# Hybrid S5 and pooling step: stores of ScalarE's results on ScalarE's queue, operands loaded one use ahead, within-chunk products over 128 rows

## The chip, the cores and the metric

The kernel runs on one core of one Trainium2 chip, in one launch. The metric is the device time in microseconds; it is given as the median of three runs. Of these runs one execution is profiled separately, and every row below comes from that execution. TensorE is called PE here, VectorE DVE, ScalarE ACT, GpSimd POOL, and SyncE, which only issues transfers, SP.

## The reference, cut to what matters

One layer works on 128 context tokens and 512 latent tokens (640 in all, D = 1024, float32). Each of 64 S5 groups has 16 channels and 64 complex states in two directions. The part that the change touches computes this:

```
z = h @ w_in + b_in                      # 1024 for S5, 512 for pooling, 2 x 1024 gates
s_t = lam_bar * s_(t-1) + B u_t          # per group, forward and backward
y   = Re(C s) + d * u                    # both directions added
v   = gelu(y_f + y_b);  v = v * sigmoid(v @ w_glu + b_glu)
yb  = pool_mix(u_b) @ w_proj_b
merged = sigmoid(g_a) * (v @ w_proj_a) + sigmoid(g_b) * yb
x = LN(alpha * x + gate * (merged @ w_out + b_out))
```

Then follow a squared-ReLU MLP with its own layer norm, and the outputs: both token sets and the final S5 states of the context.

## The kernel before

All 640 tokens go through every stage together. The S5 recurrence is cut into 80 chunks of 8 tokens (16 chunks of context, 64 of latent tokens). Per group, a matrix product brings the tokens of a chunk into a state input (`in_proj`, with weights that `gen_in` makes), a scan runs over the chunks (`scan_step`), and `out_proj` adds two parts: the state at the chunk's edge through `q`, and the influence of the tokens within the chunk on each other through `tm`. The forward direction stands in partitions 0 to 63 and the backward direction in 64 to 127, in all of these tiles. The backward half works on the chunks in reverse order, so its inputs come from a reversed copy.

The stages in order of time:

- Adaptive layer norm and the first two `w_in` blocks, up to about 45 us.
- S5 generation, about 45 to 165 us. For eight channel blocks m, PE makes the input projection (48 matmuls of 128x320), `ua_evac` lets ACT write it in chunk order to `uj`, and its reversal to `ujr`; both are stored to DRAM (`ud`, `urd`, lines 367 and 371) and loaded back with another layout (`load_u`) for `in_proj`. In between DVE makes the weights `wt` (in `gen_in`, from coefficients `b`) and `q` (in `gen_q`, from coefficients `c`), PE transposes `wt` (line 489), and `gen_t` makes `tm`, by way of DRAM (`sd`).
- Scan, about 165 to 280 us: DVE runs the scan steps, while PE computes the remaining 20 `w_in` blocks (`fill` and `plain`, line 612), whose results `g` ACT writes and SP stores (`ubd`, `gbd`, `gad`).
- Output, about 282 to 384 us: 16 calls of `out_proj(e)`, each four group columns `l`. Between them lie the last three `w_in` blocks in halves (`halves`), the pooling maps (`pool_map`) and the eight projections of the pooling branch (`pool_proj`, one per `e` from 9 on), each multiplied with a stored gate `gb`. `load_out(e + 4)` loads `tm`, `q` and `u`; `load_y` and `gelu` take the result on.
- GLU, projections, output matrix and MLP, from 384 us to the end; the change doesn't touch them.

Weights arrive as 512 KB blocks `wr` (two buffers, line 327), are split by ACT (line 321) and DVE (line 322) into a high and a low part `wh` (three buffers), and each product is made of three passes. PE writes its results to PSUM: two buffers `ps` of two banks, and four single banks.

Each engine works through its own instructions in order. A scheduler sets that order when the program is built, from the order of the code, the buffers and its own estimates; it moves loads ahead as far as their buffers allow. Before the change every transfer of this part except those of POOL is issued by SP, in one line: an issue that waits holds all that stand behind it. Transfers of SP and ACT use eight completion counters in turn, so that each also waits for the one eight places before it.

In `out_proj`, per column, two state products (real and imaginary part, `i` = 0 and 1) and the within-chunk product (`i` = 2) are each made twice, for the upper and the lower 64 rows, into two PSUM banks; the second bank is reversed in chunk order when it is added.

Of the kernel before, what the change touches and what calls it, by code (L numbers as in the profile page):

```python
# [17 lines left out]
P = 128  # L18
# [3 lines left out]
KT = 8  # L22
TC = 8
NC = NT // TC
# [14 lines left out]
def hybrid_kernel(ctx: ExitStack, tc: tile.TileContext, xin, cc, w_ada0, w_ada, w_in, w_glu, w_pa, w_pool, w_pb,  # L39
                  w_out, w_m1, w_m2, cols, rows, brow, lam, bpk, cpk, ddg, s0, cst, invc, out, nstate):  # L40
    nc = tc.nc
    V, S, T = nc.vector, nc.scalar, nc.tensor
# [318 lines left out]
    def ua_evac(m, ps):  # L361

        uj = half([P, TC, NC], "uj")
        S.activation(uj[:, ::-1, :].rearrange("p j (n c) -> p j n c", n=2),
                     v2(ps).rearrange("p n (c j) -> p j n c", j=TC),
                     AF.Identity, bias=colt[:, C_BIN + m:C_BIN + m + 1])
        dma(ud[m].rearrange("j p c -> p j c"), uj)
        ur = half([P, TC, NC], "ujr")
        S.copy(ur[:, :, 0:CP], uj[:, :, CP - 1::-1])
        S.copy(ur[:, :, CP:NC], uj[:, :, NC - 1:CP - 1:-1])  # L370
        dma(urd[m].rearrange("j p c -> p j c"), ur)

# [89 lines left out]
    us, bs = {}, [None]  # L462

    def load_u(m):
# [6 lines left out]
        return us_  # L471

    def gen_in(e):

        if e % 2 == 0:
            b = bs[0] = bt([P, 8, 3, 16], "b")
            dma(b[:, :, 0:2, :].rearrange("p (a l) r i -> p a l r i", a=2), bpk[:, e:e + 2])
            V.tensor_tensor(b[:, :, 2, :], b[:, :, 0, :], b[:, :, 1, :], op=ALU.add)
            V.tensor_tensor(b[:, :, 1, :], b[:, :, 1, :], b[:, :, 0, :], op=ALU.subtract)
# [52 lines left out]
    def gen_q(m):  # L532

        c = c3t([P, 8, 3, 16], "c")
        dma(c[:, :, 0:2, :].rearrange("p (a l) r i -> p a l r i", a=2), cpk[:, 2 * m:2 * m + 2])
        V.tensor_tensor(c[:, :, 2, :], c[:, :, 0, :], c[:, :, 1, :], op=ALU.add)
# [32 lines left out]
    def load_out(e):  # L569
# [9 lines left out]
        u = ut([P, 4, NC], "u")  # L579
        for hf, d in enumerate((ud, urd)):  # L580
            dma(u[64 * hf:64 * hf + 64], d[m, 4 * hf:4 * hf + 4].rearrange("j (i g) c -> (j i) g c", g=8)
                [:, (e % 2) * 4:(e % 2) * 4 + 4, :])
        outs[e] = q, u

    def out_proj(e):
# [5 lines left out]
        for l in range(4):  # L591
            for i in range(3):
                for hf in range(2):
                    d = slice(64 * hf, 64 * hf + 64)
                    o = pss[hf][:, l * NC:(l + 1) * NC]
                    if i < 2:
                        T.matmul(o, q[d, l, i, :], zt[d, 0:NC // 2, i, 4 * e + l, :], start=(i == 0), stop=False,  # L597
                                 skip_group_check=True)
                    else:
                        T.matmul(o, tm[d, l, e % 2, :], u[d, l, :], start=False, stop=True, skip_group_check=True)  # L600
        pf, pb = [ps[:, 0:4 * NC].rearrange("p (l c) -> p l c", l=4) for ps in pss]
# [7 lines left out]
    def plain(m, func, dst):  # L609
        ps = mm(next_w(), hx)  # L610
        g = gt([P, NT], "g")
        S.activation(tv(g), v2(ps), func, bias=colt[:, C_BIN + m:C_BIN + m + 1])  # L612
        dma(dst, g)

# [4 lines left out]
    def halves():  # L619

        while fillers:
# [7 lines left out]
            S.activation(tv(g), v2(ps), func, bias=colt[:, C_BIN + m:C_BIN + m + 1])  # L629
            dma(dst, g)  # L630
            yield
# [80 lines left out]

    def pool_proj(m):

        gb = gt([P, NT], "gb")
        dma(gb, gbd[m])
        ps = mm(wsplit(w_pb[m], 512), ybx)
        V.tensor_tensor(tv(gb), v2(ps), tv(gb), op=ALU.mult)  # L718
        dma(mbd[m], gb)
# [45 lines left out]
    for e in range(16):  # L765
# [7 lines left out]
        if e > 8:  # L773
            pool_proj(npp[0])
            npp[0] += 1
        if e % 2 == 0 and e > 3:
# [7 lines left out]
    load_y(7)  # L784
    pool_proj(7)
    gelu()
# [455 lines left out]
```

## Time and profile before

| | us |
|---|---|
| median of three runs | 1024.67 |
| lowest and highest of them | 1021.18, 1029.95 |
| the profiled execution | 1022.42 |
| span of its profile | 1020.5 |
| PE busy in the span | 980.2 |
| DVE busy | 683.5 |
| ACT busy | 410.7 |

The busy time of PE is modelled from its pipelined matmuls, so that a busy PE need not be a fast one. The granted clock is the share of PE's full clock (2.4 GHz) that the chip allowed in a stretch; the lower level is half of it. A chain of work follows the instruction that ended last back to what released it; in it an entry's length is the time until the next entry. An entry "DMA x<-y" is the time in which a transfer was under way and something waited for it.

### The profile page before, as it was taken

The page shows a single profiled execution, that of the slowest core. Times are in us where ns is not written, and L with a number is a line of the kernel's source. Part 1 is how long each engine was busy: PE and PEld are TensorE (multiplying, and loading weights), DVE is VectorE, ACT ScalarE, POOL GpSimd, SP SyncE. Part 2 cuts the span into 40 slices and gives each one's busy share as a digit, 9 for nine tenths or more (in the row PEclk, how much of TensorE's full clock was granted, in tenths as well). Part 3 has the DMA queues.
Part 4 walks back from the last instruction along what each step waited for, and adds up shares of the span by engine and source line. Part 5 has one row for each costly group of instructions (what it writes and reads, how often), then busy time and mean ns, then how long its engine had stood idle before and what let it go on. Part 6 is the DMA issues. An engine that isn't in the chain of part 4 may idle for free.

```text
span 1020.5 us, 18184 instructions
## 1 busy us (share of the span) xinstructions
PE 980.2 (96%) x7464; PEld 888.2 (87%) x7464; DVE 683.5 (67%) x1192; ACT 410.7 (40%) x687; POOL 59.5 (6%) x85
## 2 busy tenths in 40 slices
PE   4999998999999899999999999999999999999997
PEld 3898887989999799999978898889988998899886
DVE  5899878979813334546659953876855784468586
ACT  5576664322135425322243453323631364126510
POOL 0000000000285002100000001000000000000000
PEclk9999999999999999999999999999999999999998
DMA  9687666866598888867640235512232123212511
GB/s 357 218 232 205 196 199 177 223 192 189 163 287 233 223 262 302 330 202 263 232 165 21 65 107 184 130 65 73 91 106 81 53 92 105 82 42 84 185 62 62
DMA packets 116986, 166.82 MB, mean 163 GB/s; under 512 B 47720, under 2 KB 80488, under 8 KB 116904
## 3 DMA queue, kind: packets, MB, share of 16 engines
q1 hardware_dynamic: 111528, 146.27, 46.2%
q0 software_dynamic: 5376, 19.40, 5.5%
q8 instruction: 58, 0.95, 0.4%
q14 instruction: 24, 0.20, 0.1%
HBM read 135.30 MB, written 30.34 MB: 162 GB/s over the span
## 4 chain that ended last, share of the span: by engine, by line
PE 74%; DVE 10%; DMA 6%; ACT 5%; issue 4%; SPq 1%; DVEq 0%; ACTq 0%; POOLq 0%
PE ps L336 26%; PE ps L1119 16%; PE ps L1048 8%; PE psx L1048 6%; PE pse L1142 3%; PE ps L928 3%; PE psy L597 2%; PE psz L503 2%; PE pst L489 2%; PE psa L237 1%; PE ps L1142 1%; DVE wh L322 1%; DMA c<-in_cpk_dram 1%; PE psy L600 1%; ACT wh L321 1%
## 5 line engine op out<-in xcount | busy, mean ns | idle before, releaser
L336 PE MATMUL ps<-hk,wh 128*128 128x320 f32 x1344 | 213.6, 316 | 6.4 <-ACT g L612 3.0
L336 PEld LDWEIGHTS ps<-hk,wh 128*128 128x128 f32 x1344 | 200.4, 191 | 13.0 <-ACT g L612 4.3
L322 DVE TENSOR_TENSOR wh<-wr,wh 128x1024 fp32r<-128x1024 f32 (+1 forms) x113 | 128.2, 1135 | 101.7 <-ACT wh L321 100.6
L321 ACT CAST wh<-wr 128x1024 fp32r<-128x1024 f32 (+1 forms) x113 | 109.2, 966 | 170.6 <-PE ps L1119 91.9
L1119 PE MATMUL ps<-wh,fx 128*128 128x512 f32 x720 | 164.2, 389 | 0.0
L1119 PEld LDWEIGHTS ps<-wh,fx 128*128 128x128 f32 x720 | 134.9, 188 | 27.8
L336 PEld LDWEIGHTS ps<-gx,wh 128*128 128x128 f32 x384 | 56.4, 187 | 3.3 <-issue 2.9
L336 PE MATMUL ps<-gx,wh 128*128 128x320 f32 x384 | 58.7, 310 | 0.0
L336 PEld LDWEIGHTS ps<-vx,wh 128*128 128x128 f32 x384 | 56.4, 188 | 2.5 <-ACT sg L852 2.1
L336 PE MATMUL ps<-vx,wh 128*128 128x320 f32 x384 | 58.1, 311 | 0.0
L1048 PE MATMUL psx<-h,wh 128*128 128x320 f32 x288 | 47.6, 308 | 0.0
L1048 PE MATMUL ps<-h,w 128*128 128x320 f32 x288 | 46.5, 307 | 0.0
L1048 PEld LDWEIGHTS psx<-h,wh 128*128 128x128 f32 x288 | 43.7, 187 | 0.2
L1048 PEld LDWEIGHTS ps<-h,w 128*128 128x128 f32 x288 | 43.2, 187 | 0.0
L612 ACT ACTIVATE g<-ps,colt 128x640 f32<-128x640 f32 x17 | 13.5, 794 | 71.4 <-PE ps L336 71.4
L890 DVE TENSOR_TENSOR ps<-ps,gate 128x512 f32<-128x512 f32 (+2 forms) x39 | 28.1, 748 | 21.1 <-PE ps L1119 16.1
L597 PE MATMUL psy<-zt,q 64*128 64x80 f32 x512 | 41.4, 273 | 0.0
L597 PEld LDWEIGHTS psy<-zt,q 64*128 64x128 f32 x512 | 35.0, 188 | 3.1 <-issue 2.9
L928 PE MATMUL ps<-wo,mx 128*128 128x512 f32 x150 | 36.6, 392 | 0.2 <-ACT wo L321 0.2
L336 PE MATMUL ps<-ybx,wh 128*128 128x320 f32 x192 | 32.5, 329 | 3.5 <-DVE gb L718 3.1
L336 PEld LDWEIGHTS ps<-ybx,wh 128*128 128x128 f32 x192 | 30.6, 203 | 4.4 <-issue 3.2
L225 POOL DMA_DIRECT2D wa<-in_w_ada_dram x32 | 16.9, 532 | 295.1 <-PE psa L237 110.3
(267 smaller groups left out, 1604.1 us busy)
## 6 DMA issues: line engine op xcount, KB each, us to landing
wr<-in_w_m_dram SPq DMA_DIRECT2D x64, 512.0 KB
wa<-in_w_ada_dram POOLq DMA_DIRECT2D x32, 512.0 KB, 5.9
wr<-in_w_in_dram SPq DMA_DIRECT2D x28, 512.0 KB
qd<-q SPq DMA_DIRECT2D x8, 1024.0 KB
q<-qd SPq DMA_DIRECT2D x16, 512.0 KB
x<-in_xin_dram SPq DMA_DIRECT2D x10, 512.0 KB
wa<-in_w_ada_dram SPq DMA_DIRECT2D x10, 512.0 KB
tm<-sd SPq DMA_DIRECT2D x8, 512.0 KB
```

The costliest lines, as they stand in the source:

```text
L225: nc.gpsimd.dma_start(w, w_ada[self.mod, :, k * D:(k + 1) * D])
L321: S.copy(hi, raw)
L322: V.tensor_tensor(lo, raw, hi.bitcast(F32), op=ALU.subtract)
L336: T.matmul(ps[:, n, 0:ln], hl[:, wh, k * P:(k + 1) * P], xk[:, xh, o:o + ln], start=(k == 0 and i == 0), stop=(k == nk - 1 and i == 2))
L489: T.transpose(ps[:, i * P:(i + 1) * P], wt[:, 2 * h + i // 2, i % 2, :], ident)
L503: T.matmul(ps[64 * d:64 * d + 64, o:o + NC], w[:, 2 * h + l, r, 64 * d:64 * d + 64], us[m][d][:, (e % 2) * 4 + 2 * h + l, :], start=True, ...
L597: T.matmul(o, q[d, l, i, :], zt[d, 0:NC // 2, i, 4 * e + l, :], start=(i == 0), stop=False, skip_group_check=True)
L890: V.tensor_tensor(ps, ps, g[:, c0:c1], op=ALU.mult)
L928: T.matmul(ps[:, n, :], mx[k][:, xh, t * P:(t + 1) * P], wo[k][:, wh, n * 512:(n + 1) * 512], start=(k == 0 and i == 0), stop=(k == KT - 1 ...
L1048: T.matmul(ps, hl[:, wh, c + k * P:c + (k + 1) * P], rq[b][:, xh, k, :], start=(start and k == 0 and i == 0), stop=(stop and k == 3 and i ...
L1119: T.matmul(pt[t], fx[k][:, xh, t * P:(t + 1) * P], hl[:, wh, kk * 512:(kk + 1) * 512], start=(k == 0 and i == 0), stop=(k == 7 and i == 2))
L1142: T.matmul(ps[n][:, 0:ln], fx[k][:, xh, t * P:(t + 1) * P], hl[:, wh, o_:o_ + ln], start=(k == 0 and i == 0), stop=(k == 7 and i == 2))
```

## The change

Four edits in one:

- The stores of `uj` and `ujr` and of the gates and pooling inputs `g` (36 stores in all) are issued by ACT, which writes these tiles, and no longer by SP.
- The coefficients `b` and `c` are loaded by `load_b` and `load_c`, called one use ahead of the code that needs them.
- `load_proj` loads the gate `gb` and splits the weight block of a pooling projection one `e` before `pool_proj` uses them.
- The within-chunk product of `out_proj` is one product over all 128 rows of `tm` and `u` into the first bank. `u` is now loaded from `ud` alone, in one transfer.

```diff
@@ ua_evac
-        dma(ud[m].rearrange("j p c -> p j c"), uj)
+        nc.scalar.dma_start(ud[m].rearrange("j p c -> p j c"), uj)
...
-        dma(urd[m].rearrange("j p c -> p j c"), ur)
+        nc.scalar.dma_start(urd[m].rearrange("j p c -> p j c"), ur)
...
+    def load_b(e):
+        b = bt([P, 8, 3, 16], "b")
+        dma(b[:, :, 0:2, :].rearrange("p (a l) r i -> p a l r i", a=2), bpk[:, e:e + 2])
+        nextb.append(b)
+    def load_c(m):
+        c = c3t([P, 8, 3, 16], "c")
+        dma(c[:, :, 0:2, :].rearrange("p (a l) r i -> p a l r i", a=2), cpk[:, 2 * m:2 * m + 2])
+        nextc.append(c)
+    load_b(0)
+    load_c(0)
...
         if e % 2 == 0:
-            b = bs[0] = bt([P, 8, 3, 16], "b")
-            dma(b[:, :, 0:2, :].rearrange("p (a l) r i -> p a l r i", a=2), bpk[:, e:e + 2])
+            b = bs[0] = nextb.pop(0)
+            if e < 14:
+                load_b(e + 2)
...
-        c = c3t([P, 8, 3, 16], "c")
-        dma(c[:, :, 0:2, :].rearrange("p (a l) r i -> p a l r i", a=2), cpk[:, 2 * m:2 * m + 2])
+        c = nextc.pop(0)
+        if m < KT - 1:
+            load_c(m + 1)
@@ load_out
-        for hf, d in enumerate((ud, urd)):
-            dma(u[64 * hf:64 * hf + 64], d[m, 4 * hf:4 * hf + 4].rearrange("j (i g) c -> (j i) g c", g=8)
-                [:, (e % 2) * 4:(e % 2) * 4 + 4, :])
+        dma(u, ud[m].rearrange("j (i g) c -> (j i) g c", g=8)[:, (e % 2) * 4:(e % 2) * 4 + 4, :])
@@ out_proj
         for l in range(4):
-            for i in range(3):
+            for i in range(2):
                 for hf in range(2):
                     d = slice(64 * hf, 64 * hf + 64)
-                    o = pss[hf][:, l * NC:(l + 1) * NC]
-                    if i < 2:
-                        T.matmul(o, q[d, l, i, :], zt[d, 0:NC // 2, i, 4 * e + l, :], start=(i == 0), stop=False,
-                                 skip_group_check=True)
-                    else:
-                        T.matmul(o, tm[d, l, e % 2, :], u[d, l, :], start=False, stop=True, skip_group_check=True)
+                    T.matmul(pss[hf][:, l * NC:(l + 1) * NC], q[d, l, i, :], zt[d, 0:NC // 2, i, 4 * e + l, :],
+                             start=(i == 0), stop=(hf == 1 and i == 1), skip_group_check=True)
+            T.matmul(pss[0][:, l * NC:(l + 1) * NC], tm[:, l, e % 2, :], u[:, l, :], start=False, stop=True,
+                     skip_group_check=True)
@@ plain, halves
-        dma(dst, g)
+        nc.scalar.dma_start(dst, g)
...
-    def pool_proj(m):
-        gb = gt([P, NT], "gb")
-        dma(gb, gbd[m])
-        ps = mm(wsplit(w_pb[m], 512), ybx)
+    def load_proj():
+        m = npp[0]
+        npp[0] += 1
+        gb = gt([P, NT], "gb")
+        dma(gb, gbd[m])
+        prep.append((m, gb, wsplit(w_pb[m], 512)))
+    def pool_proj():
+        m, gb, hl = prep.pop(0)
+        ps = mm(hl, ybx)
...
         if e > 8:
-            pool_proj(npp[0])
-            npp[0] += 1
+            pool_proj()
+        if 7 < e:
+            load_proj()
```

What the scheduler makes of it, at three places. First PE at the start of `out_proj(0)`, two columns: `psy` are the two PSUM banks, `zt,q` a state product, `u,tm` a within-chunk product. Before:

```order
L597 MATMUL psy_3706<-zt,q_3617 128x80
L597 MATMUL psy_3707<-zt,q_3617 128x80
L597 MATMUL psy_3706<-zt,q_3617 128x80
L597 MATMUL psy_3707<-zt,q_3617 128x80
L600 MATMUL psy_3706<-u_3619,tm_3615 128x80
L600 MATMUL psy_3707<-u_3619,tm_3615 128x80
L597 MATMUL psy_3706<-zt,q_3617 128x80
L597 MATMUL psy_3707<-zt,q_3617 128x80
L597 MATMUL psy_3706<-zt,q_3617 128x80
L597 MATMUL psy_3707<-zt,q_3617 128x80
L600 MATMUL psy_3706<-u_3619,tm_3615 128x80
L600 MATMUL psy_3707<-u_3619,tm_3615 128x80
```

After:

```order
L610 MATMUL psy_3702<-zt,q_3617 128x80
L610 MATMUL psy_3703<-zt,q_3617 128x80
L610 MATMUL psy_3702<-zt,q_3617 128x80
L610 MATMUL psy_3703<-zt,q_3617 128x80
L612 MATMUL psy_3702<-u_3619,tm_3615 128x80
L610 MATMUL psy_3702<-zt,q_3617 128x80
L610 MATMUL psy_3703<-zt,q_3617 128x80
L610 MATMUL psy_3702<-zt,q_3617 128x80
L610 MATMUL psy_3703<-zt,q_3617 128x80
L612 MATMUL psy_3702<-u_3619,tm_3615 128x80
```

Each column has one product instead of two for `u,tm`, and the state products of the next column follow it. Over the whole program, PE's order goes from a product over 128 rows to products over 64 rows in this stage, and back, 16 times before and 67 times after.

Second, DVE where the last two weights `wt` of S5 generation and the fourth `q` are made (`c_1920` before and `c_1559` after are the coefficients of that `q`; the `c` row near the end prepares the next coefficients loaded into the buffer that these free). Before:

```order
L564 TENSOR_TENSOR sq_1914<-psq_1881,dd 128x2x16
L541 TENSOR_TENSOR c_1920<-c_1920 128x8x16
L566 TENSOR_TENSOR sq_1914<-sq_1914,psq_1881 128x2x16
L454 TENSOR_TENSOR q_1923<-pqt,c_1920 128x8x128
L455 TENSOR_TENSOR q_1923<-oy_1929,q_1923 128x8x128
L459 TENSOR_TENSOR q_1923<-q_1923,oy_1929 128x8x128
L452 TENSOR_TENSOR oy_1941<-pws,b_1936 128x512
L536 TENSOR_TENSOR c_2470<-c_2470 128x8x16
L455 TENSOR_TENSOR wt_1940<-oy_1941,wt_1940 128x4x128
L457 TENSOR_TENSOR wt_1940<-wt_1940,oy_1941 128x4x128
```

After:

```order
L583 TENSOR_TENSOR sq_1918<-sq_1918,psq_1885 128x2x16
L455 TENSOR_TENSOR q_1927<-oy_1933,q_1927 128x8x128
L558 TENSOR_TENSOR c_1559<-c_1559 128x8x16
L453 TENSOR_TENSOR wt_1942<-pwt,b_1732 128x4x128
L454 TENSOR_TENSOR q_1927<-pqt,c_1559 128x8x128
L454 TENSOR_TENSOR wt_1942<-pwt,b_1732 128x4x128
L459 TENSOR_TENSOR q_1927<-q_1927,oy_1933 128x8x128
L452 TENSOR_TENSOR oy_1943<-pws,b_1732 128x512
L455 TENSOR_TENSOR wt_1942<-oy_1943,wt_1942 128x4x128
L457 TENSOR_TENSOR wt_1942<-wt_1942,oy_1943 128x4x128
L553 TENSOR_TENSOR c_2180<-c_2180 128x8x16
L452 TENSOR_TENSOR oy_1987<-pws,b_1732 128x512
```

Between the last reader of the old coefficients (`L454` of `q`) and the row on the new ones stand three rows before and five after, and the weights `wt_1942` are complete ahead of that row, where `wt_1940` were not.

Third, SP in the output stage, around the first loads of a stored gate (`gb<-gbd`), with the `q` load of e = 14 (`q_4389` before, `q_4338` after). Before:

```order
L605 DMA yd<-y_4281 128x320
L575 DMA tm_4387<-sd 128x8x128
L578 DMA q_4389<-qd 128x1024
L727 DMA yn_4279<-yd 128x8x80
L716 DMA gb_4317<-gbd 128x640
L605 DMA yd<-y_4356 128x320
L581 DMA u_4391<-ud 64x320
L581 DMA u_4391<-urd 64x320
L716 DMA gb_4394<-gbd 128x640
```

After:

```order
L618 DMA yd<-y_4239 128x320
L597 DMA u_4268<-ud 128x320
L592 DMA tm_4336<-sd 128x8x128
L618 DMA yd<-y_4309 128x320
L595 DMA q_4338<-qd 128x1024
L597 DMA u_4340<-ud 128x320
L733 DMA gb_4230<-gbd 128x640
L749 DMA yn_4237<-yd 128x8x80
L733 DMA gb_4297<-gbd 128x640
L733 DMA gb_4369<-gbd 128x640
L741 DMA mbd<-gb_4230 128x640
L327 DMA wr_4504<-in_w_pb_dram 128x512
```

In both orders the first `gb` load stands behind the `q` load of e = 14; after, the store of out_proj(10)'s `y` (`y_4309`) and the `u` load of e = 14 stand ahead of it too, and three gates are then loaded close together. In PE's order the third pooling projection now follows after two instead of 24 products of out_proj(11).

## Rows read from the trace of the kernel before

**Rows 1.** The page's busy times: us, share of the span, instructions.

```profile
PE 980.2 (96%) x7464; PEld 888.2 (87%) x7464; DVE 683.5 (67%) x1192; ACT 410.7 (40%) x687; POOL 59.5 (6%) x85
```

**Rows 2.** Table of stretches: busy us and count by engine, granted clock, DMA share.

```profile
core 0: us, PE busy (x) PEld busy (x) DVE busy (x) ACT busy (x) POOL busy (x), PEclk, DMA share, GB/s
150.00:160.00 10.00, 5.69 (x77) 4.11 (x75) 6.60 (x11) 3.97 (x9) 0.00 (x0) 0.83 0.47 130
210.00:220.00 10.00, 8.17 (x78) 7.90 (x60) 8.75 (x30) 4.09 (x9) 0.00 (x0) 0.83 0.54 174
350.00:360.00 10.00, 6.88 (x50) 6.76 (x47) 3.76 (x6) 4.25 (x5) 0.00 (x0) 0.66 0.79 249
45.00:384.00 339.00, 323.01 (x3359) 304.34 (x3360) 238.47 (x524) 151.66 (x308) 41.70 (x44) 0.97 0.75 212
```

**Rows 3.** Waits of PE: who for whom, us in total, times, longest.

```profile
PE pst L489 <- DVE wt L455: 6.5, 4, 4.3
PE ps L336 <- DVE gb L718: 3.1, 1, 3.1
PE ps L336 <- ACT g L612: 3.0, 2, 1.8
```

**Rows 4.** Chain of work, 146 to 156 us: start, length, what.

```profile
146.82 1.17 DVE q L454
...
148.05 6.24 DMA c<-in_cpk_dram
...
154.60 0.61 DVE wt L455
155.22 0.04 issue
155.26 0.69 PE pst L489 x2
```

**Rows 5.** Chain of work from 203 us, then DVE in order of time.

```profile
203.44 7.09 DMA wr<-in_w_in_dram
...
210.56 1.05 ACT wh L321
...
210.88 0.29 DVE L524 TENSOR_TENSOR ta<-lmr,zt 128x128 f32<-128x128 f32 x1 [4.08 <-DMA out_dram<-last]
```

**Rows 6.** SP in order of time: start, us of the issue, line, transfer.

```profile
181.31 3.94 SPq L613 DMA_DIRECT2D ubd<-g  x1
...
193.65 3.52 SPq L613 DMA_DIRECT2D gbd<-g  x1
...
198.80 2.60 SPq L613 DMA_DIRECT2D gbd<-g  x1
201.49 1.86 SPq L543 DMA_DIRECT2D qd<-q  x1
203.44 3.16 SPq L327 DMA_DIRECT2D wr<-in_w_in_dram  x1
```

**Rows 7.** Chain of work, 340 to 356 us.

```profile
342.07 2.69 SPq L578
...
345.28 8.36 DMA gb<-gbd
...
353.73 0.83 DVE gb L718
354.57 0.14 issue
354.70 1.41 PE ps L336 x4
```

**Rows 8.** Chain of work, 260 to 295 us: projections (L336), state (L597), chunk products (L600).

```profile
260.67 21.35 PE ps L336 x144
...
287.54 3.71 PE ps L336 x24
291.25 0.60 PE psy L597 x8
291.86 0.22 PE psy L600 x4
292.08 0.45 PE psy L597 x8
...
294.09 3.71 PE ps L336 x24
```

**Rows 9.** Chain of work, 134 to 140 us: state inputs, 128 rows, 80 columns.

```profile
139.21 1.26 PE psz L503 x32
```

**Rows 10.** SP's issue of a `uj` store; the group of ACT's `g` (page).

```profile
109.79 0.38 SPq L367 DMA_DIRECT2D ud<-uj  x1
...
L612 ACT ACTIVATE g<-ps,colt 128x640 f32<-128x640 f32 x17 | 13.5, 794 | 71.4 <-PE ps L336 71.4
```

More of the change, by code (lines that the diff above doesn't have):

```diff
@@ L471, in load_u @@
         return us_
+    nextb, nextc = [], []
+    def load_b(e):
[8 more added lines that the diff above has]
+    load_c(0)
     def gen_in(e):
         if e % 2 == 0:
-            b = bs[0] = bt([P, 8, 3, 16], "b")
-            dma(b[:, :, 0:2, :].rearrange("p (a l) r i -> p a l r i", a=2), bpk[:, e:e + 2])
+            b = bs[0] = nextb.pop(0)
+            if e < 14:
+                load_b(e + 2)
             V.tensor_tensor(b[:, :, 2, :], b[:, :, 0, :], b[:, :, 1, :], op=ALU.add)
@@ L629, in halves @@
             S.activation(tv(g), v2(ps), func, bias=colt[:, C_BIN + m:C_BIN + m + 1])
-            dma(dst, g)
+            nc.scalar.dma_start(dst, g)
             yield
@@ L711, in pool_map @@
         ybx.append(yb)
-    def pool_proj(m):
+    prep = []
+    def load_proj():
+        m = npp[0]
+        npp[0] += 1
         gb = gt([P, NT], "gb")
         dma(gb, gbd[m])
-        ps = mm(wsplit(w_pb[m], 512), ybx)
+        prep.append((m, gb, wsplit(w_pb[m], 512)))
+    def pool_proj():
+        m, gb, hl = prep.pop(0)
+        ps = mm(hl, ybx)
         V.tensor_tensor(tv(gb), v2(ps), tv(gb), op=ALU.mult)
@@ L784, in hybrid_kernel @@
     load_y(7)
-    pool_proj(7)
+    pool_proj()
     gelu()
```

## The prediction

> **What bounds the kernel now.** I read the busy times first. TensorE (PE) works 980.2 us of a span of 1020.5, so PE's own work and the holes in it make the time [rows 1]. The table of stretches comes next, because the change touches only the part from the second channel group's evacuation to the gate projections, about 45 to 384 us. There PE is busy 323.0 of 339 us at a mean granted clock of 0.97 [rows 2]. So 16 us of that part are holes, and 0.03 x 339 = 10 us more are work done at half clock. About 26 us is all that better feeding could ever return; any other gain has to take work off PE.
>
> The list of waits and the chain of work say which holes these are. The transposes of `wt` wait for DVE 6.5 us, 4.3 of it at once; a gate projection waits 3.1 for DVE's product with `gb`; two projections wait 3.0 for ScalarE (ACT) [rows 3]. Three of them matter. Between 148.05 and 155.26 DVE waits for a coefficient load `c` of 6.24 us, and behind it in DVE's order stand the `wt` rows that PE transposes next [rows 4]. At 203.44 the load of a `w_in` block is issued late and lands 7.09 us later, and ACT's cast only starts at 210.56 [rows 5]; PE then stands still for 1.8 us [rows 3], and DVE for 4.08 us behind the small store `last` [rows 5]. At 345.28 the load of `gb` takes 8.36 us and PE's next projection starts at 354.70 [rows 7]. After each the clock is granted at its lower level (1.2 GHz) for a while: 0.83 over 150 to 160 and over 210 to 220, which costs 1.7 us each, and 0.66 over 350 to 360, which costs 3.4 us [rows 2].
>
> **Products over 128 rows.** Before, the within-chunk product is two products of 64 rows on the two row halves; they start together, as the four state products ahead of them do. Four group columns take 0.45 us (state) and 0.22 us (chunk) each [rows 8]. A block of 24 projection matmuls and four such columns repeats every 6.55 us (287.54 to 294.09). At the pace without changes, 21.35 us for 144, the 24 matmuls take 3.56, and four columns take 4 x 0.67 = 2.68, in all 6.24. The 0.31 us left over are the price of one visit to the 64-row shape and back [rows 8]; it also shows directly: the first eight state products after a projection take 0.60 instead of 0.45, and the 24 projections behind take 3.71 instead of 3.56.
>
> After the change every column goes from 64-row state products to one 128-row product and back. In the order of PE before there are 16 visits to the 64-row shape in this stage, in the order after there are 67. The 51 new ones cost 51 x 0.31 = 15.8 us. What is saved: a full-height stream of 80 columns takes 0.069 us (32 `psz` products, 16 pairs, take 1.26 us, less half a visit, 0.155) [rows 9], so two passes take 0.14 instead of 0.22, and 64 columns save 64 x 0.08 = 5.1 us. Net +10.7 us. Bounds: if a full-height product is no quicker than the pair, nothing is saved, +15.8; if this particular pair of shapes can be mixed freely, only the saving is left, -5.1. I take +10.7, because shape changes of every kind that the trace holds cost about the same, and in this stage PE has almost no holes that could swallow it.
>
> The Trainium skill, "TensorEngine Tiling (Array Packing)", Key Properties, says that changing the tiling mode drains TensorE, while a change of tile within a mode does not. By it the change pays at each of the 128 steps in and out; by the saving alone the sum would be 5.1 us lower than now instead of 10.7 higher. The trace agrees with the rule: 0.31 us for each visit [rows 8].
>
> The new order also has four more visits to the column shapes (`psz`, `psq`) in the S5 generation stage, 4 x 0.31 = +1.2 us. Sixteen half-size loads of `u` from `urd` go; SP's queue is shorter by them, which counts below.
>
> **Coefficients one use ahead.** These loads come with two buffers, and the scheduler already hoists them as far as the buffers allow. The load that DVE waits for at 148.05 starts the moment DVE's last reader of the buffer ends (`q` L454, 146.82 + 1.17), not when the program reaches it [rows 4]. In the order after, the same holds: the load of `c_2180` takes the buffer of `c_1559`, read last by the `q` L454 six rows ahead of the waiting row. What changes is how much DVE has to do between: 2.9 us of rows before, 3.5 us after (rows of 0.6 and 1.14 us). So I count -0.7 us for this edit, bounds 0 and the whole hole, 4.3 + 1.7 = -6.0. I stay near zero because the limit is the buffer. The half clock at 155 stays.
>
> **Stores on ACT's queue.** SP's stores of ScalarE's results stand in one line with the loads. Some hold it long: 3.94 us at 181.31, 3.52 at 193.65 and 2.60 at 198.80, and behind them the `w_in` load is issued at 203.44 [rows 6]. Without the two `gbd` stores SP reaches that load when DVE has freed the buffer, about 202.2, and issues it without the 3.16 us; even with 4 to 5 us to land ACT can cast at about 207. The 1.8 us hole and the 1.7 us of half clock then go: up to -3.5, and I take -3.0. The bound on the other side is 0. On ACT each issue costs what SP pays for an unhindered one, 0.38 us [rows 10]: 36 x 0.38 = 14 us of ACT time. It lies in ACT's idle time: ACT is busy 151.7 of the 339 us [rows 2], and before each `g` it has waited 71.4/17 = 4.2 us for PE [rows 10]. I price it at 0, bound +3.
>
> **Projection operands one use ahead.** The store and load order of SP decides. Before, `gb` of the first projection stands behind the `q` load of e = 14, which waits 2.69 us for out_proj(10) [rows 7]. After, it stands behind the same `q` load, and besides behind that step's `y` store and `u` load. So it isn't issued earlier in SP's order. PE's third projection, the one that waits, now comes 22 products earlier, after two products of out_proj(11). In favour: out_proj(10) is complete earlier in PE's order, with most of out_proj(11) and two projections between it and the wait. The time from the end of out_proj(10) to the wait is 3.3 (18 products of out_proj(11)) + 8.1 (54 projection matmuls at 0.15) + 0.4 = about 12 us of PE work; `gb` needs some 4 us to be issued, 5 to 8.4 us to land and 0.83 for DVE's product [rows 7], 10 to 13 us. The hole shrinks from 3.1 us to about 1, and with it, probably, the lower clock: of 3.1 + 3.4 = 6.5 us I take -4.0, bounds 0 and -6.5.
>
> **Sum.** The profiled execution took 1022.42 us, 2.2 below the median of 1024.67. 1022.4 + 10.7 + 1.2 - 0.7 - 3.0 - 4.0 + 0 = 1026.6 us.
>
> **Rivals.**
> - *Shapes mix freely.* The 128-row product joins the stream without a gap, so the PE term is -5.1 and the time is 1022.4 - 5.1 - 0.7 - 7.0 = 1009.6, faster. Against it: 0.31 us at every visit of the trace [rows 8]. It decides if a visit costs under 0.12 us. Chance 0.10.
> - *The feeding gains are larger.* If nearly all 26 us of holes and half clock go, say 20, the time is 1022.4 + 11.9 - 20 = 1014.3. Against it: the `wt` holes are DVE's own work and buffers. Chance 0.06, half of it below 1%.
> - *ACT is held instead of SP* (the side of slower). All DMAs of SP and ACT take eight counters in turn, and each waits for the DMA eight places back. In the new order the `ubd` and `gbd` stores on ACT wait so for SP's `q`, `tm` and `qd` transfers, which land late here; ACT's casts of weights and its reading of PSUM stand behind. SP was held up to 3.94 us [rows 6]; ACT has 4.2 us of cover before a `g` [rows 10]. If six of the 20 `g` stores hold ACT 1 us beyond the cover and the feeding gains are lost, the time is 1022.4 + 11.9 + 6 = 1040. It decides once ACT is held over 4 us at a store. Chance 0.13.
> - *The loads land no sooner.* The load at 203.44 took 7.09 us [rows 5] with the DMA engines busy 0.75 of the part [rows 2]; if the transfers themselves are the limit, -3.0 and -4.0 fall away and the time is 1033.6, still within 1%. Chance 0.14. The Trainium skill, "DMA: Bandwidth & Descriptors", on issuing engines not being separate queues, says that DMAs from several engines share the same 16 DMA engines, and that a second issuer only saves issue time. By that rule the time is that of this rival; no run here yet shows a DMA issued by ACT.
>
> **Numbers.** Forecast chance 0.57 (1019 to 1033). The bound of "no change" is 1%, about what a measurement of this kernel can tell: 1014.4 to 1034.9. Faster: 0.10 + 0.03; slower: 0.13 and 0.01 of the forecast's edge; the rest, 0.73, is within 1%. The range from 1012 to 1036 leaves out the free mixing and the worse half of the held ACT.
>
> **What would show it.** In the changed trace: four state products and one chunk product of a column take about 0.9 us instead of 0.67, and the out_proj part gets some 10 us longer per PE. The wait of DVE for `c` near 150 is still there at 2 to 3 us. The `w_in` load near 203 is issued before 203 and lands before 208, and PE has no hole near 210. The `gb` hole is near 1 us. ACT shows no idle time behind a store beyond 1 us. I am wrong if a column stays at or under 0.67 us, or if new holes of PE end with ACT.

## The result and the profile after

The changed kernel takes 1034.49 us (median of 8 runs) beside 1025.52 us for the kernel before: a ratio of 1.0105, 95% interval 1.0067 to 1.0143. That is slower, by 10.8 us (7 to 15). The prediction was 1026.6 us, "no change"; the time lies inside its range, near the upper end, but the loss is clear of noise, and none was forecast. The profiled execution took 1035.45 us. Some runs of the kernel before, 15 of the 89 beside which the experiments below are set, have a mean granted clock of 0.98 instead of 0.99 and take about 8 us longer, so that an average moves with the number of such runs in it.

Busy times of the page of after (us, share of the span, instructions), as [rows 1] of before:

```profile
span 1033.5 us, 17896 instructions
PE 992.8 (96%) x7336; PEld 891.8 (86%) x7336; DVE 683.2 (66%) x1192; ACT 411.3 (40%) x687; POOL 59.1 (6%) x85
```

The span grew by 13.0 us and PE's busy time by 12.6. So the loss looks like work on PE and not like holes. The table of stretches of after, as [rows 2]:

```profile
core 0: us, PE busy (x) PEld busy (x) DVE busy (x) ACT busy (x) POOL busy (x), PEclk, DMA share, GB/s
45.00:384.00 339.00, 323.72 (x3127) 297.24 (x3126) 235.24 (x519) 150.25 (x305) 41.27 (x44) 0.99 0.71 206
150.00:160.00 10.00, 10.00 (x98) 9.09 (x98) 9.93 (x16) 4.34 (x13) 0.00 (x0) 1.00 0.40 110
210.00:220.00 10.00, 10.00 (x126) 9.61 (x125) 7.72 (x30) 4.46 (x10) 0.00 (x0) 1.00 0.71 232
350.00:360.00 10.00, 10.00 (x82) 8.55 (x82) 3.64 (x7) 4.14 (x7) 0.00 (x0) 1.00 0.86 233
200.00:205.00 5.00, 4.64 (x21) 4.68 (x22) 5.00 (x13) 1.04 (x1) 0.00 (x0) 0.66 0.53 116
```

The three places that the edits were aimed at are healed: PE has no hole in them and the granted clock is 1.00 where it was 0.83, 0.83 and 0.66. The last row is a new loss: 0.66 behind a wait of PE for `sq`. Yet PE is busy 323.7 of the 339 us, as it was before (323.0). The list of waits of PE in after (for whom, us in total, times, longest) shows why:

```profile
PE psz L519 <- DMA u<-ud: 5.6, 3, 2.4
PE ps L336 <- DVE sq L583: 4.3, 3, 2.8
PE psq L574 <- DVE q L455: 1.7, 1, 1.7
PE ps L336 <- ACT g L625: 1.2, 1, 1.2
PE pst L505 <- DVE wt L455: 1.2, 2, 0.6
PE psz L519 <- DMA u<-urd: 0.7, 2, 0.4
```

And the same list of before has one more row that is wanted here:

```profile
PE ps L336 <- DVE sq L566: 1.5, 2, 0.8
```

Gone, against [rows 3]: 5.3 us of `pst`, 1.8 of `g`, 3.1 of `gb`. Come: 6.3 us of `psz` for the loads of `u`, 2.8 of `sq`, 1.7 of `psq` (in the list of before, which goes down to 0.2 us, neither `psz` nor `psq` stands). That is 10.2 us gone and 10.8 come. The holes have moved; they have not shrunk.

Two cuts of the span tell where the 13 us lie. The chain of work of after, as [rows 8], gives the start of the output stage behind its x144 block, and the steps of that stage:

```profile
264.23 21.35 PE ps L336 x144
...
293.44 3.56 PE ps L336 x24
297.00 0.60 PE psy L610 x8
297.61 0.38 PE psy L612 x2
...
300.94 1.07 PE ps L336 x7
```

The stage ends where the first product with `vx` starts. PE's group on that tile (count, shortest/median/longest ns, first and last start), in before and in after:

```profile
L336 PE MATMUL ps<-vx,wh x384: 305/309/416, 391.0 to 455.2; 128*128 128x320 f32 x192
```

```profile
L336 PE MATMUL ps<-vx,wh x384: 305/309/416, 403.2 to 467.4; 128*128 128x320 f32 x192
```

The output stage starts at 264.23 + 21.35 = 285.6 instead of 282.0 [rows 8], 3.6 us later. It lasts 403.2 - 285.6 = 117.6 us instead of 391.0 - 282.0 = 109.0, 8.6 us more. The remaining 0.8 us lie behind. A column takes 0.60 + 0.38 = 0.98 us instead of 0.67, and a block of 24 projections and four columns 300.94 - 293.44 = 7.50 instead of 6.55. Sixteen such blocks make 15.2 us. The `gb` hole of 3.1 us and the 3.4 of half clock behind it are gone from the stage, which leaves 8.7.

### The profile page after: what moved, and what is told of

Its sections match the earlier page's. It is cut to its first block, busy times and chain, and to the rows that moved or that the text cites. A ratio compares the mean times of both kernels' runs of the same rounds, so it can differ in the third digit from the quotient of the medians.

```text
span 1033.5 us, 17896 instructions
## 1 busy us (share of the span) xinstructions
PE 992.8 (96%) x7336; PEld 891.8 (86%) x7336; DVE 683.2 (66%) x1192; ACT 411.3 (40%) x687; POOL 59.1 (6%) x85
## 4 chain that ended last, share of the span: by engine, by line
PE 72%; DVE 12%; DMA 7%; issue 4%; ACT 4%; SPq 0%; DVEq 0%; ACTq 0%; POOLq 0%
PE ps L336 24%; PE ps L1142 16%; PE ps L1071 8%; PE psx L1071 6%; PE psy L610 4%; PE pse L1165 3%; PE ps L951 3%; PE psy L612 2%; DVE wh L322 2%; PE psa L237 1%; PE psz L519 1%; DMA u<-urd 1%; PE ps L1165 1%; DVE zt L543 1%; DVE ta L540 1%
## 5 line engine op out<-in xcount | busy, mean ns | idle before, releaser
L336 PE MATMUL ps<-hk,wh 128*128 128x320 f32 x1344 | 211.4, 315 | 7.5 <-DVE sq L583 4.3
L336 PEld LDWEIGHTS ps<-hk,wh 128*128 128x128 f32 x1344 | 199.7, 190 | 14.1 <-issue 5.5
L336 PEld LDWEIGHTS ps<-gx,wh 128*128 128x128 f32 x384 | 56.4, 187 | 3.3 <-issue 2.9
L336 PE MATMUL ps<-gx,wh 128*128 128x320 f32 x384 | 58.7, 310 | 0.0
L336 PEld LDWEIGHTS ps<-vx,wh 128*128 128x128 f32 x384 | 56.4, 188 | 2.5 <-ACT sg L875 2.1
L336 PE MATMUL ps<-vx,wh 128*128 128x320 f32 x384 | 58.1, 311 | 0.0
L610 PE MATMUL psy<-zt,q 64*128 64x80 f32 x512 | 44.1, 285 | 0.0
L951 PEld LDWEIGHTS ps<-wo,mx 128*128 128x128 f32 x150 | 27.9, 188 | 6.5 <-ACT wo L321 0.9
L519 PE MATMUL psz<-u,w 128*64 128x80 f32 x512 | 26.9, 239 | 6.3 <-DMA u<-ud 5.6
```

The costliest lines, as they stand in the source:

```text
L336: T.matmul(ps[:, n, 0:ln], hl[:, wh, k * P:(k + 1) * P], xk[:, xh, o:o + ln], start=(k == 0 and i == 0), stop=(k == nk - 1 and i == 2))
L519: T.matmul(ps[64 * d:64 * d + 64, o:o + NC], w[:, 2 * h + l, r, 64 * d:64 * d + 64], us[m][d][:, (e % 2) * 4 + 2 * h + l, :], start=True, ...
L610: T.matmul(pss[hf][:, l * NC:(l + 1) * NC], q[d, l, i, :], zt[d, 0:NC // 2, i, 4 * e + l, :], start=(i == 0), stop=(hf == 1 and i == 1), s ...
L951: T.matmul(ps[:, n, :], mx[k][:, xh, t * P:(t + 1) * P], wo[k][:, wh, n * 512:(n + 1) * 512], start=(k == 0 and i == 0), stop=(k == KT - 1 ...
```

## The experiments

The first theory, **V**, was that the visits to the 64-row shape are the loss. It put 0.40 us on a visit, because a column had become 0.31 us longer although the 128-row product was thought to save 0.08. Against it stood **P**, that the 128-row product is slow by itself, and **S**, that the stores on ACT's queue cost something. After the first runs **W** was added: a visit is the price, and the 128-row product takes as long as its pair. Each kernel was timed beside the kernel before on the same chip. The first column of us is the distance of the ratio from 1, times 1022. The second is the difference of the means of those runs alone that have a mean granted clock of 0.989 or more, and how many of the kernel's runs these are.

| kernel | what of the change it has | ratio to before (95%) | us | us, clock 0.989 or more |
|---|---|---|---|---|
| the change | all four edits | 1.0105 (1.0067 to 1.0143) | +10.7 | not on record |
| e1 | 128-row products alone | 1.0104 (1.0055 to 1.0153) | +10.6 | +10.0 (5 of 6) |
| e2 | the other three | 1.0040 (1.0004 to 1.0075) | +4.1 | +0.8 (7 of 12) |
| e3 | all, products grouped | 0.9976 (0.9948 to 1.0005) | -2.5 | -1.3 (12 of 12) |
| e5 | 128-row products alone, grouped | 0.9939 (0.9915 to 0.9964) | -6.2 | -4.9 (12 of 12) |
| e4 | stores on ACT alone | 1.0029 (0.9995 to 1.0064) | +3.0 | -0.7 (5 of 12) |
| e10 | stores of `uj`, `ujr` alone | 1.0007 (0.9982 to 1.0033) | +0.7 | +0.1 (10 of 12) |
| e9 | stores of `g` alone | 1.0013 (0.9982 to 1.0044) | +1.3 | -0.3 (8 of 12) |
| e6 | coefficients ahead alone | 0.9983 (0.9951 to 1.0015) | -1.7 | -2.6 (10 of 12) |
| e7 | projections' operands ahead alone | 0.9998 (0.9965 to 1.0031) | -0.2 | -0.7 (8 of 11) |
| e11 | all, loads of `u` on POOL's queue | 1.0080 (1.0051 to 1.0109) | +8.2 | +8.5 (8 of 8) |
| e13 | e3 with the loads of `u` on POOL's queue | 0.9937 (0.9911 to 0.9964) | -6.4 | -4.9 (12 of 12) |
| e12 | e5, `uj` stores on ACT, `u` loads on POOL | 0.9927 (0.9897 to 0.9958) | -7.5 | -6.7 (7 of 7) |

Spans, stages and waits are those of one execution of each kernel. Runs of the kernel before at a clock of 0.989 or more lie between 1017.0 and 1025.5 us, so a few us between two profiles count only where rows show what they consist of.

**One edit and its complement (e1, e2).** e1 is the kernel before with the new loop and the single load of `u`; e2 is the changed kernel with the old ones. In the diff of the change these are its parts `out_proj` and `load_out`, taken alone or left out.

> The kernel before with the within-chunk product over 128 rows alone (u from ud in one load). In the changed kernel's trace a column takes 0.60 + 0.38 = 0.98 us instead of 0.67. Theory V (each visit to the 64-row shape and back costs 0.40 us): 51 more visits are 20.4 us, 64 columns save 0.086 each, 5.5 us, so about 15 us over before, ratio near 1.014, and the whole loss of the change is in this edit. Rival S (the loss comes from the stores on ScalarE's queue, and the slower columns take the place of holes): ratio 1.000 to 1.005.

> The changed kernel with the within-chunk product as before, two products of 64 rows, so stores on ScalarE, coefficients and projection operands ahead remain. Theory V: 1034.5 less about 15 us, that is about 1020, ratio to before near 0.995. Rival S: the loss stays, ratio 1.008 to 1.012.

e1 alone loses as much as the whole change, and e2 is not the gain that was counted: where 0.7% faster was forecast, it is 0.4% slower over all its runs and 0.8 us slower over the seven at the higher clock. In e1's profile the step is that of after, and the stage takes 399.6 - 279.9 = 119.7 us:

```profile
279.90 0.61 PE psy L593 x8
280.50 0.38 PE psy L595 x2
```

```profile
L336 PE MATMUL ps<-vx,wh x384: 305/309/416, 399.6 to 463.8; 128*128 128x320 f32 x192
```

In e2's waits of PE the `u` loads are there, which before has none of, and the `gb` hole is down to 1.0 us:

```profile
PE psz L519 <- DMA u<-ud: 3.2, 3, 1.3
PE psz L519 <- DMA u<-urd: 2.3, 2, 1.9
PE ps L336 <- DVE sq L583: 2.1, 2, 1.1
```

**The visits taken away (e3, e5).** The same products in another order: the state products of four columns first, then their four 128-row products. e3 is the change so edited, e5 the kernel before with this alone.

```diff
         for l in range(4):
             for i in range(2):
                 for hf in range(2):
...
-                             start=(i == 0), stop=(hf == 1 and i == 1), skip_group_check=True)
-            T.matmul(pss[0][:, l * NC:(l + 1) * NC], tm[:, l, e % 2, :], u[:, l, :], start=False, stop=True,
-                     skip_group_check=True)
+                             start=(l == 0 and i == 0), stop=(hf == 1 and i == 1), skip_group_check=True)
+        for l in range(4):
+            T.matmul(pss[0][:, l * NC:(l + 1) * NC], tm[:, l, e % 2, :], u[:, l, :], start=False, stop=True,
+                     skip_group_check=True)
```

> The changed kernel, but in each out_proj the state products of all four columns come first and the four 128-row products behind them, so that a call has one visit to the 64-row shape instead of four. Theory V: 48 or more visits of 0.40 us go, 19 to 20 us less than the changed kernel: about 1015, ratio near 0.990. Rival P (the 128-row product costs 0.38 us by itself, not by the change of shape): no change, 1034, ratio 1.010.

> The kernel before with edit 4 alone (128-row within-chunk products, whole loads of u), but in another order: the state products of the four columns of a step first, then the four 128-row products, so PE visits the 64-row shape once a step as before. V (a visit in and out of the 64-row shape is the price, and a 128-row product takes half the time of the pair): 5.1 us faster than before, 0.995. W (a visit is the price, but a 128-row product takes as long as the pair of 64-row ones, 0.22 us a column): no change in the steps, 0.998 to 1.002 (1024.67 us for 1024.67), by a step of 6.55 us in the output stage. If the half-size loads of u hold SP, up to 0.5% faster by that.

Grouping takes back 13.2 us of the change (1.0105 - 0.9976) and 16.9 of e1 (1.0104 - 0.9939). Between the profiles it is 14.7 (1033.5 - 1018.8) and 14.6 (1029.0 - 1014.4), and 48 visits at 0.31 us are 14.9. So P falls: the same 64 products of 128 rows are all still there. But V's 0.990 for e3 is not reached either. The chain of work of e5 says which of its two figures was wrong:

```profile
280.11 1.95 PE psy L593 x32
...
283.10 1.94 PE psy L593 x32
285.05 1.05 PE psy L596 x8
286.10 3.56 PE ps L336 x24
289.65 1.95 PE psy L593 x32
```

The block is 289.65 - 283.10 = 6.55 us, exactly that of before. The eight passes of the four 128-row products take 1.05 us. The 24 projections behind are back at 3.56, so the way out of the visit (0.15) lies in the 1.05. That leaves 0.90 / 8 = 0.112 us for a pass, and 0.22 for a column, as long as the pair of 64-row products took [rows 8]. Nothing is saved. The visit is then 0.31 us as predicted, and the column of after adds up: 0.45 + 0.22 + 2 x 0.155 = 0.98. W holds. The order in which the accumulation falls on the same part of PSUM is hardly another explanation: before, the pairs accumulated on a column just written too, and at 0.22 us.

What does set the pace of a pass? With 64 rows a pass of 128 output columns takes as long: the state products' 0.45 us are four passes of a pair, 0.112 each [rows 8]. Each pass has a weight load (PEld) of its own, of 128 columns here and of 64 in the `psz` pairs of [rows 9], and in e5 the loads are busy in nearly all of the 1.05 us (PEld in order of time). That the loads set the pace would fit; no run tries it.

```profile
284.98 0.97 PEld L596 LDWEIGHTS psy<-u,tm 128*128 128x128 f32 x8
```

Still e5 is 6.2 us faster than before (4.9 at the higher clock), and no part of that is PE's step. Its output stage takes 384.4 - 280.1 = 104.3 us instead of 109.0. PE's list of waits has no `gb` any more. Why, the group of SP's issues of `gb` shows (count, shortest/median/longest ns, first and last start; then the time to landing):

```profile
L713 SPq DMA_DIRECT2D gb<-gbd x5: 377/443/1657, 340.9 to 359.3; - x5
...
DMA to landing us min/median/max: 5.2/5.6/6.1
```

```profile
L336 PE MATMUL ps<-vx,wh x384: 305/309/416, 384.4 to 448.7; 128*128 128x320 f32 x192
```

`gb` is issued from 340.9 instead of 345.28 and lands within 6.1 us instead of 8.36 [rows 7]. The half-size loads of `u` from `urd` that stood ahead of it in SP's line are not there. That they are what held it is argued from this order and not shown: no run drops them alone, and the orders of PE and SP differ in other places too.

**The stores on ACT (e4, e10, e9).** e4 moves all 36, e10 the 16 of `uj` and `ujr`, e9 the 20 of `g`; each edit is one of these lines:

```diff
-        dma(ud[m].rearrange("j p c -> p j c"), uj)
+        nc.scalar.dma_start(ud[m].rearrange("j p c -> p j c"), uj)
...
-        dma(dst, g)
+        nc.scalar.dma_start(dst, g)
```

> The kernel before with the 36 stores of ScalarE's results on its own queue and nothing else. The prediction's step: 3 to 3.5 us faster, ratio 0.997, TensorE without a hole near 210. Rival S: slower, ratio 1.004 to 1.010, with TensorE waiting for loads of u in the generation stage (2.3 us holes as in the changed kernel's trace).

> The kernel before with the stores of uj and ujr alone on ScalarE's queue (16 DMAs); the stores of g stay on SP. S (with those stores off SP's line, other loads and stores come ahead of the u loads, which psz then waits for): holes of PE ended by u<-ud or u<-urd near 90, 120 and 138 us, 3 to 6 us in all, as in the changed kernel; time 1.000 to 1.004. If the stores of g are what moves the u loads, no such holes, 0.997 to 1.000.

> The kernel before with the stores of g alone on ScalarE's queue (20 DMAs). As predicted: the load of the w_in block near 203 is issued without the hold and lands by 208, the hole of 1.8 us near 210 and its half clock go, 3.0 us less, 0.997. Rival (the loads land no sooner): 1.000. S for the u loads: none of PE's holes ends with u here, since the stores of uj stay in SP's line.

None is faster. The +3.0 us of e4 are no loss to be explained either: seven of its twelve runs have a mean clock of 0.98, beside 3 of 29 of before, and the other five are 0.7 us faster than before. Whether the stores bring that clock about, or chance does, no run tells. In e4's profile the output stage starts at 278.6 us, 3.4 earlier than before: PE's waits for `wt` fall from 6.5 us to 0.8, and 4.1 us of waits for `u` have come. Behind that start the gain is lost again (span 1019.8 us against 1020.5). In e10 PE's waits for `u` come with these 16 stores alone, in e9 they are absent:

```profile
PE psz L503 <- DMA u<-urd: 2.7, 2, 1.9
...
PE psz L503 <- DMA u<-ud: 1.6, 1, 1.6
```

e9 shows the predicted step and its end. The store takes ACT 0.33 us, and the `w_in` block is cast at 208.00, not 210.56 [rows 5]. But PE then waits for another such cast, 1.9 us instead of 1.8, up to 219.13; the old hole ended at 212.35. ACT in order of time, and a row of PE's waits, both of e9:

```profile
204.62 0.33 ACTq L613 DMA_DIRECT2D gbd<-g  x1
208.00 1.05 ACT L321 CAST wh<-wr 128x1024 fp32r<-128x1024 f32 x1 [3.41 <-DMA wr<-in_w_in_dram]
```

```profile
PE ps L336 <- ACT wh L321: 1.9, 1, 1.9
```

**Operands ahead (e6, e7).** Each edit alone; the diff is that of the change (`load_b` and `load_c`; `load_proj` and `pool_proj`).

> The kernel before with the coefficients b and c asked for one use ahead alone. As predicted (the loads hang on the buffer): 0.7 us less, 0.999 to 1.000, DVE's wait for c near 150 stays at 2 to 4 us. Rival (the loads do come earlier): DVE's wait for c near 150 and the half clock behind it go, 0.994 to 0.996. S (a load put ahead in SP's line pushes the loads behind it): a new wait of DVE or PE for b or u of 1 to 5 us, 1.000 to 1.003.

> The kernel before with the projections' operands loaded one use ahead alone. As predicted: the hole of 3.1 us at gb and the half clock behind it shrink by 4.0 us, 0.996, psy to vx 105 us instead of 109. S (a load moved ahead pushes another one back in SP's line): the hole is gone but another load is late by as much, 0.999 to 1.002.

e6 can't be told from the -0.7 us forecast, and DVE's wait for `c` is still there, as the buffer argument had it (DVE in order of time, e6):

```profile
150.79 0.29 DVE L553 TENSOR_TENSOR c<-c 128x128 f32<-128x128 f32 x1 [3.30 <-DMA c<-in_cpk_dram]
```

But its profile shows more than the forecast. The output stage starts at 277.0 us instead of 282.0, and PE's holes of before near 112 (1.7 us) and 212 (1.8 us) are not there, which the forecast for this edit did not touch (PE in order of time, before; then the group of state products, e6):

```profile
112.28 0.41 PE L489 MATMUL pst<-ident,wt 128*128 128x128 f32 x2 [1.69 <-DVE wt L455]
```

```profile
L614 PE MATMUL psy<-zt,q x512: 267/268/335, 277.0 to 378.9; 64*128 64x80 f32 x171
```

What the edit alone is worth stays open, between -5 and +1.5 us.

In e7 the `gb` wait is gone from the list and the output stage takes 387.5 - 282.5 = 105.0 us instead of 109.0, the -4.0 of the forecast. Yet the span is only 1.6 us shorter and the time unchanged. In e7 PE waits 2.8 us for `sq` instead of 1.5 and 0.9 for a cast of `wh` instead of 0.4; what is behind the stage takes 1.9 us more (1018.9 - 387.5, against 1020.5 - 391.0).

```profile
PE ps L336 <- DVE sq L566: 2.8, 3, 1.3
```

**The loads of `u` out of SP's line (e11, e13).** In the changed kernel SP issues the `u` loads like this (SP in order of time, after; start, us of the issue):

```profile
130.34 2.84 SPq L469 DMA_DIRECT2D u<-ud  x1
133.27 1.17 SPq L469 DMA_DIRECT2D u<-urd  x1
134.53 1.15 SPq L469 DMA_DIRECT2D u<-ud  x1
...
136.28 0.44 SPq L477 DMA_DIRECT2D b<-in_bpk_dram  x1
```

They hold SP for 5.6 us, and the load of `b` is issued only behind them. DVE then waits 5.2 us for it, and later 4.2 for `c` (DVE in order of time, after):

```profile
144.33 0.29 DVE L494 TENSOR_TENSOR b<-b 128x128 f32<-128x128 f32 x1 [5.20 <-DMA b<-in_bpk_dram]
```

In before the wait was this one (DVE in order of time, before):

```profile
154.31 0.29 DVE L536 TENSOR_TENSOR c<-c 128x128 f32<-128x128 f32 x1 [3.33 <-DMA c<-in_cpk_dram]
```

So the wait of 3.3 us for `c` that ended at 154 has gone, and one of 5.2 for `b` that ends at 144 stands in its place. The edit that tests it, on the changed kernel (e11) and on e3 (e13):

```diff
-            dma(u, d[m].rearrange("j (i g) c -> (j i) g c", g=8))
+            nc.gpsimd.dma_start(u, d[m].rearrange("j (i g) c -> (j i) g c", g=8))
```

> The changed kernel with the loads of u (the S5 input, two for each second step) issued by GpSimd's queue instead of SP's. S (the u loads are late because of what stands ahead of them in SP's line): the holes of psz near 90, 121 and 137 us, 5.6 us in all, go, and the time is 4 to 6 us below the changed kernel's, 1.004 to 1.007 of before. Rival (the u loads are late because the transfers themselves or the stores on ScalarE are late): the holes stay, 1.009 to 1.011.

> The changed kernel with the four columns' products grouped and the u loads on GpSimd's queue. V with S (visits and late u loads are the whole loss): the changed kernel's 1.0105 less 14.7 us of visits and 5.2 of u holes, 0.991 of before. Rival (the other edits lose elsewhere): 0.997 to 1.000, as the grouped one without the move of the u loads.

No wait for `u` is left in e11, and its output stage starts at 259.00 + 21.35 = 280.4 instead of 285.6, 5.2 us earlier, of which 0.8 are there already ahead of PE's first wait for `u`. From e3 to e13 the start moves from 284.1 to 279.2, 5.0 us. But e13's output stage then takes 108.3 us instead of 103.8, with waits of PE of 2.2 us for `gb` and 1.9 for `ph`. These are the two largest rows of PE's waits in e11 behind the first, which lies outside the stretch:

```profile
PE ps L336 <- DVE sq L583: 4.2, 3, 2.2
PE pst L505 <- DVE wt L455: 2.3, 2, 1.6
```

DVE's wait for `b` shrinks to 3.26 us in e11. The timed gain is smaller than the profile's: 2.6 us from the change to e11 and 4.0 from e3 to e13, both with intervals that overlap. That the loads of `u` were late in SP's line is shown; what made SP hold them longer with the stores on the other queue is not. The stores and loads of both queues share counters of completion, and the order on SP is another one; no run tells these two apart.

**Beyond both kernels (e12).** e5 with the `uj` stores on ACT and the `u` loads on POOL.

> A candidate beyond both kernels: the grouped 128-row products alone (0.994 of before), and with them the stores of uj and ujr on ScalarE's queue and the loads of u on GpSimd's, so that SP's line holds neither. S (the u loads in SP's line are what made the stores' move worthless): the holes of PE near 110 and 150 go as they did with the stores moved, and no u holes come: 4 to 7 us below the grouped kernel, 0.987 to 0.990. Rival (the wait only moves on, to b or to the casts): 0.992 to 0.996.

With 0.9927 it is the fastest kernel measured, but not apart from e5 (0.9939) or e13 (0.9937). Its further moves are worth 1.2 us as measured, which the intervals can't tell from nothing. The profile agrees with the rival's reading that the wait moves on: no wait for `u` is left and the output stage starts at 279.6 instead of e5's 280.1, but it takes 107.3 us instead of 104.3. There PE waits 1.4 us for a cast, and the clock of the 5 us behind is 0.66 (PE in order of time, e12):

```profile
364.75 0.85 PE L336 MATMUL ps<-ybx,wh 128*128 128x320 f32 x4 [1.42 <-ACT wh L321]
```

This execution took 1018.63 us, the second longest of seven, so the profile may show e12 at its worse end. The gain is in the main that of e5.

## Why the prediction was wrong

The forecast was a sum of +11.9 us for PE and -7.7 for the feeding, +4.2 in all. The profiles give +16.4 for PE (15.2 in the output stage and the 1.2 counted ahead of it), and with a span 13.0 us longer that leaves -3.4 for the feeding. Two steps failed: the 5.1 us that the 128-row products were to save, which are nothing, and the 3.7 us that stores and coefficients were to gain ahead of the output stage, where 7.1 us of holes went and 10.8 came. It is luck that the time still fell into the range: the hole at `gb` closed whole, 6.5 us instead of the 4.0 counted.

- **51 visits x 0.31 = +15.8: right.** A column takes 0.98 us (forecast: about 0.9), a block 0.95 more, and 48 visits fewer return 13 to 17 us as timed, 14.6 and 14.7 in the profiles. The rule of the Trainium skill, "TensorEngine Tiling (Array Packing)", Key Properties, that a change of the tiling mode drains the engine, agrees with this: e1 and e5 differ only in the order of the products, and so in how often the shape changes, and by 1.65%.
- **64 x 0.08 = -5.1 saved: wrong, it is 0.** This is the term that was mis-sized. I took 0.069 us for a 128-row pass from the `psz` pairs [rows 9]. Those are two products with 64 output columns each, side by side. The product that the edit makes has 128 output columns and takes 0.112 a pass, no less than the pair that it replaces; [rows 8] had this price, 0.112 for a state pass of 128 output columns. My own upper bound, "if a full-height product is no quicker than the pair", was the case.
- **"SP's queue is shorter by them, which counts below": never counted.** Without the sixteen loads e5's output stage is 4.7 us shorter (104.3 against 109.0), and they are the likely reason. The two errors cancel by luck, and so the edit alone measures +10.6 us where +10.7 was forecast.
- **Coefficients -0.7: right in its reason, open in size.** In the edit alone (e6) the wait for `c` hangs on the buffer as argued, but two other holes go with it, and the time is -1.7 (-5 to +1.5). "The wait of DVE for `c` near 150 is still there" fails in the changed kernel, where a longer wait for `b` stands ahead of it.
- **Stores -3.0: wrong, no gain came.** Alone +3.0 (-0.5 to +6.5), or -0.7 in the runs at the higher clock; the `uj` half +0.7, the `g` half +1.3. The hole near 210 did go, as forecast. But I asked only what the stores hold up on SP, and not which loads move up or back in SP's order once they are gone. The loads of `u`, which no hole of before ended with, became the last to come: 6.3 us of PE's waits. In after the `w_in` load is issued at 206.56, not ahead of 203.

```profile
206.56 1.33 SPq L327 DMA_DIRECT2D wr<-in_w_in_dram  x1
```

- **Projections' operands -4.0: right in its stage, but not in the total.** The hole and its half clock go in e7 and in the change. But alone e5 and e1 lose the hole too, so in the change it is not a second gain: the shorter line of SP and the earlier load close the same hole.
- **The rivals.** "ACT is held instead of SP" is not what made the loss: most stores take ACT 0.33 to 0.42 us, and PE waits less for `g` than before (1.2 against 3.0). Its sign shows in two places all the same, where ACT stands idle 1.7 us behind a `uj` store near 53 and 1.5 at an `ubd` store near 185, until SP's load of `tm` has landed. The nearest was "the loads land no sooner" at 1033.6, but by luck: its reason, that the transfers themselves are the limit, is not what the runs show, since the hole at `gb` closed and the loads of `u` came in time from another queue (e11). The rule that I set beside it, in the Trainium skill, "DMA: Bandwidth & Descriptors", on issuing engines not being separate queues, agrees with e4, e9 and e10, none faster. e11 and e13 show what a second issuer can do: take loads out of a line that holds them.

Put together, from the profiles: up to the start of the output stage +6.3, +2.8 and +1.7 of new holes and +1.2 for the added visits, less 5.3 and 1.8 of holes and about 1.7 of half clock (three such stretches before; two after, one at 200 and one near 25 us, ahead of what the change touches; each as in the rows at 150 and 200), make +3.2 of the 3.6 us; in the output stage 15.2 - 6.5 = +8.7 of 8.6.

## What to carry to other kernels

Price a change of shape by the number of times that the order goes in and out of it, and group the products of one shape before making them taller; and take a pass's duration only from a product with the same rows, output columns and moving columns. When transfers leave a queue, write down what then stands at its head: a hole closed in one place is a gain only if the next load in that line is early. Of two edits that close the same hole, count one.

## What was not expected of the hardware

A product over 128 rows with 80 moving columns in f32 took the same 0.22 us as two products of 64 rows that run side by side (e5). The clock: in the profile of e9 a wait of PE of 1.4 us for `ph` near 325 is followed by a granted clock of 0.50 over more than 20 us, in which PE is busy nearly throughout (table of stretches, e9):

```profile
330.00:340.00 10.00, 10.00 (x76) 9.05 (x76) 2.46 (x6) 2.77 (x6) 0.00 (x0) 0.50 0.72 176
325.00:355.00 30.00, 28.92 (x191) 26.29 (x192) 9.43 (x18) 13.73 (x22) 0.00 (x0) 0.54 0.68 185
```

The same is in e10 at the same place, and not in e13, where PE waits 1.9 us for `ph` there and the clock stays at 1.00:

```profile
330.00:340.00 10.00, 9.93 (x103) 8.75 (x102) 5.47 (x10) 4.88 (x9) 0.00 (x0) 1.00 0.91 221
```

So neither the length of a hole nor its place tells the cost of the lower level (1.2 GHz) behind it; here it was 0.46 x 30 = 13.8 us where the other holes of this case cost 1.7 or 3.4. It lifts the spans of e9 and e10 above that of before, while their timed ratios, 1.0013 and 1.0007, can't be told from 1, so that their spans are not read here. The two executions have a mean clock of 0.982 and 0.981, the twelve others that were profiled 0.989 to 0.997, so the longer runs at 0.98 probably hold such a stretch. What sets it was not tried.
